# A fifth Strassen pair and three held pairs in the second FFN product of a two-layer trunk

## The chip, the core and the metric

The kernel runs on one core of one Trainium2 chip. The engines of a core work side by side, each on its own instruction stream: TensorE (PE; PEld is its weight load), VectorE (DVE), ScalarE (ACT), GpSimd (POOL), and SyncE (SP), which here issues the weight transfers. Matmul results go to eight banks of PSUM; everything else stands in SBUF. The metric is the device time of one execution in microseconds, as the median of several runs.

## What is computed

Two layers, each of three blocks on x of 256 tokens by 1024 channels, in float32:

```
for l in range(DEPTH):                                   # DEPTH = 2
    h = _swiglu(x, ffn_w1[l, 0], ffn_w3[l, 0], ffn_w2[l, 0])
    x = _layernorm(ALPHA * x + 0.5 * h, ln_g[l, 0], ln_b[l, 0])
    h = _mixer(x, ...)
    x = _layernorm(ALPHA * x + h, ln_g[l, 1], ln_b[l, 1])
    h = _swiglu(x, ffn_w1[l, 1], ffn_w3[l, 1], ffn_w2[l, 1])
    x = _layernorm(ALPHA * x + 0.5 * h, ln_g[l, 2], ln_b[l, 2])
```

with `_swiglu(x, w1, w3, w2) = (silu(x @ w1) * (x @ w3)) @ w2` and an inner width of 2816. The mixer (a gated spatial unit and differential attention, merged by gates) isn't touched by the change; what matters of it is that it starts, like an FFN, with a matrix product of the new x.

So there are four FFNs. Three of them hand their result to a next stage: to the mixer, to the next layer's first FFN, to the mixer again. The fourth ends the kernel.

## The kernel before

**Number format.** Every float32 operand is split into hi and lo: ACT copies it to the rounded type fp32r (hi), DVE subtracts hi from it (lo). A product then takes three matmuls, x_hi w_hi, x_hi w_lo and x_lo w_hi (`three`, L208). Weights arrive by DMA in pieces of 1 MB into `raw` (four buffers) and are split into `hi` and `lo` (eight buffers of 1024 columns each) by `stream` (L150). With `lent`, a half of a piece goes to slots of the activation pool instead (31 slots of 512 columns, the pool `act`), in splits of `sub` columns.

**An FFN** (L551) has two parts. The first makes the inner activations: four of the 22 k tiles (tiles of 128 inner channels) by `front`, the other 18 by `gemm_a2` in a loop over pairs of k tiles (L596). Inner tiles are kept as hi and lo, or, for pairs in `SQ`, go through `mixed` (L559), which adds and subtracts their 128 by 128 quarters for Strassen's form and splits the seven results.

The second part multiplies by w2 to 256 tokens by 1024 channels, in four blocks (t, c): token half t, channel half c. It goes by pairs of k tiles:

- a *plain pair* (`PQ`, `rows_p`): two k tiles in four blocks, three matmuls of 128x512 each. One `rows_p` call does one pair in one block, six matmuls;
- a *Strassen pair* (`SQ`, `stream_s` and L632): two k tiles, two token halves and two channel halves form a two by two block product, which takes seven block products S1 to S7 instead of eight, three matmuls each. `stream_s` (L280) forms the sums of weight blocks in place in `raw` (L306, L308, L309, on DVE) and splits seven blocks of 512 columns (`cut`, L289). Two pairs share one buffer for S1's weights.

Before the change there are four Strassen pairs and seven plain ones (`NS = 4`). The loop at L629 does a Strassen pair and, behind the first three, a plain pair. Then the sums of S1, S5, S6 and S7 go into the residual (L636 to L645, DVE), and the four plain pairs left are *held*: all are split into the eight `hi` and `lo` buffers, and the loop at L648 goes block by block, (0, 0), (0, 1), (1, 0), (1, 1), through all held pairs, so that a token half is done before the other.

**The normalization** (`Norm`, L434) follows each block: `part` adds a block to the residual, `finish(t, ...)` computes mean and variance of a token half and normalizes it on DVE (the last instruction is noted in `ends[t]`). For each half h of the channels, `turn(t, h)` (L528) then transposes on PE (L532), scales on ACT (L538) and splits the next stage's x on ACT and DVE (L540). For t = 0 and h = 1 DVE's part of the split is queued behind `ends[1]`, if that is set already.

**The order.** PE's instructions run in the order in which the program is traced. The other engines' order comes from a scheduler by priorities; `behind(ins)` puts an instruction behind `ins` on the same engine. Where PE does a transpose for a task is set by a beat counter: `beat(w)` (L123) is called with 0.5 for every `rows_p` or `rows_b` call and starts the tasks that are due; `finish` registers its task, which counts from the beat after it.

```
yield waits[h]            # turned(t, waits), L517
self.turn(t, h)
...
beat(n / 1024)            # rows_p, L258
...
ln.finish(t, ((2, 1.5), (2, 1))[t])      # the FFN, L655
```

**The next stage** begins with `gemm_b2` (L317): pieces of weights in steps of two k tiles (`rows_b`, six matmuls each), for t = 0 and then t = 1; x's first half (h = 0) is read by the first four steps, the second by the next four. Its four weight pieces are streamed with `lent = [(0, 1), (0,), (), ()]`, so that three halves go to slots.

## Time and profile before

| | us |
|---|---|
| median of 3 runs (1230.62 to 1231.16) | 1230.86 |
| the profiled execution | 1231.23 |
| its span, first to last instruction | 1229.5 |
| `wlo` splits on DVE (L171), 410 in all | 450.0 busy |
| `slo` splits on DVE (L295), 64 in all | 69.3 busy |
| sums of weight blocks on DVE (L306, L308, L309) | 19.6, 11.0, 11.0 busy |

Times are from the profile of one execution on the chip. In a row of a group, the name of the line and engine comes first, then the result and the operands, the shape and the count; behind the bar stand the time in which the engine was busy with the group, the mean of one in ns, and the idle time of the engine just before them with what ended it. In the timeline and in the chain of work that ended last, a row begins with its start and its length in us. In the table by stretches of time, each engine has its busy time and its number of instructions. Matmuls overlap, so a matmul's own length (390 ns) is more than the distance from one to the next.

### The profile page before, as it was taken

How to read it: one execution, taken by the hardware profiler on the slowest of the kernel's cores; microseconds unless marked ns; L12 is line 12 of the kernel's file. 1: busy time of each engine (PE TensorE's matmuls, PEld its weight loads, DVE VectorE, ACT ScalarE, POOL GpSimd, SP SyncE). 2: the span in 40 equal slices, each digit the busy share in tenths (PEclk: the TensorE clock that was granted, in tenths of full speed). 3: DMA queues.
4: the chain of work that ended last, by engine and by line, in shares of the span. 5: the costliest groups of instructions: out<-in, count | busy, mean ns of one | idle time of the engine just before them, and what ended most of it. 6: DMA issues, size and time to landing. Idle time of an engine off the chain costs nothing.

```text
span 1229.5 us, 17890 instructions
## 1 busy us (share of the span) xinstructions
PE 1223.3 (99%) x6589; PEld 1050.6 (85%) x6589; DVE 980.3 (80%) x1692; ACT 781.1 (64%) x1424; POOL 87.0 (7%) x184
## 2 busy tenths in 40 slices
PE   9999999999999999999999999999999999999998
PEld 8888888888888888888888888888888888888886
DVE  6877998886587987779978779978866879787886
ACT  6775666679665666656566665566886555766651
POOL 0100000244100000000000000002430000000000
PEclk9999999999999999999999999999999999999999
DMA  9864665654754745546645546656556446455450
GB/s 344 291 205 138 231 217 194 224 167 166 251 178 154 231 159 207 191 138 241 247 178 196 180 142 247 246 188 206 168 174 229 168 171 240 171 206 178 160 211 34
DMA packets 40104, 241.87 MB, mean 197 GB/s; under 512 B 5281, under 2 KB 6353, under 8 KB 13393
## 3 DMA queue, kind: packets, MB, share of 16 engines
q1 hardware_dynamic: 36048, 227.82, 53.2%
q0 software_dynamic: 3536, 12.13, 3.1%
q8 instruction: 51, 0.84, 0.3%
q10 hardware_dynamic: 432, 0.79, 0.2%
q14 instruction: 37, 0.30, 0.1%
HBM read 235.47 MB, written 1.05 MB: 192 GB/s over the span
## 4 chain that ended last, share of the span: by engine, by line
PE 99%; DMA 0%; DVE 0%; ACT 0%; DVEq 0%; issue 0%; ACTq 0%
PE bank L223 38%; PE bank L211 23%; PE bank L230 20%; PE sbank L211 12%; PE bank L371 2%; PE sbank L707 1%; PE sbank L532 1%; PE sbank L756 1%; PE sbank L837 1%; DMA xraw<-in_xT 0%; PE sbank L754 0%; PE sbank L778 0%; PE sbank L585 0%; PE sbank L741 0%; PE sbank L746 0%; PE sbank L504 0%
## 5 line engine op out<-in xcount | busy, mean ns | idle before, releaser
L171 DVE TENSOR_TENSOR wlo<-raw,whi 128x1024 fp32r<-128x1024 f32 (+1 forms) x410 | 450.0, 1116 | 109.1 <-PE bank L230 62.9
L169 ACT ACTIVATE whi<-raw 128x1024 fp32r<-128x1024 f32 (+1 forms) x410 | 388.8, 970 | 186.9 <-PE bank L223 114.8
L223 PE MATMUL bank<-x,whi 128*128 128x512 f32 x1792 | 426.5, 392 | 0.0
L223 PEld LDWEIGHTS bank<-x,whi 128*128 128x128 f32 x1792 | 330.7, 188 | 69.1 <-issue 2.7
L230 PE MATMUL bank<-x,wlo 128*128 128x256 f32 x1792 | 230.0, 284 | 0.0
L230 PEld LDWEIGHTS bank<-x,wlo 128*128 128x128 f32 x1792 | 224.2, 191 | 4.8
L231 ACT ACTIVATE r<-bank 128x256 f32<-128x256 f32 x256 | 96.0, 381 | 67.8 <-PE bank L230 67.4
L211 PE MATMUL bank<-whi,x 128*128 128x512 f32 x328 | 106.6, 394 | 0.0
L293 ACT ACTIVATE shi<-raw 128x1024 fp32r<-128x1024 f32 (+1 forms) x64 | 60.4, 950 | 61.0 <-DVE raw L309 39.1
L295 DVE TENSOR_TENSOR slo<-raw,shi 128x1024 fp32r<-128x1024 f32 (+1 forms) x64 | 69.3, 1088 | 24.8 <-PE bank L230 15.3
L211 PEld LDWEIGHTS bank<-whi,x 128*128 128x128 f32 x328 | 61.6, 188 | 12.7
L211 PE MATMUL sbank<-whi,hhi 128*128 128x512 f32 x168 | 65.7, 391 | 0.0
L211 PE MATMUL sbank<-whi,hlo 128*128 128x512 f32 x168 | 65.4, 389 | 0.0
L211 PE MATMUL sbank<-wlo,hhi 128*128 128x512 f32 x168 | 65.4, 389 | 0.0
L211 PE MATMUL bank<-wlo,x 128*128 128x512 f32 x164 | 64.0, 390 | 0.0
L538 ACT ACTIVATE xf<-sbank,ln_b,ln_g 128x128 f32<-128x128 f32 x80 | 30.1, 456 | 40.8 <-PE sbank L532 40.8
L233 DVE TENSOR_TENSOR silu<-bank,r 128x256 f32<-128x256 f32 x144 | 54.5, 418 | 0.4
L431 POOL DMA_DIRECT2D bc<-in_lng x6 | 3.2, 530 | 728.4 <-DVE bc L430 728.4
L683 POOL TENSOR_TENSOR swap<-swap,sin_t 128x512 f32<-128x512 f32 x16 | 25.0, 1563 | 233.4 <-DMA swap<-z 225.2
L211 PE MATMUL bank<-lhi,x 128*128 128x512 f32 x120 | 39.2, 395 | 0.0
L211 PEld LDWEIGHTS sbank<-whi,hlo 128*128 128x128 f32 x168 | 31.5, 188 | 6.7
L211 PEld LDWEIGHTS sbank<-wlo,hhi 128*128 128x128 f32 x168 | 31.6, 188 | 6.5
(236 smaller groups left out, 1682.3 us busy)
## 6 DMA issues: line engine op xcount, KB each, us to landing
raw<-in_w13a SPq DMA_DIRECT2D x72, 1024.0 KB, 4.9
raw<-in_w2p SPq DMA_DIRECT2D x28, 1024.0 KB, 5.1
raw<-in_wa SPq DMA_DIRECT2D x24, 1024.0 KB, 5.2
raw<-in_w2s SPq DMA_DIRECT2D x16, 1024.0 KB, 4.9
raw<-in_wb SPq DMA_DIRECT2D x16, 1024.0 KB, 5.0
raw<-in_wqk SPq DMA_DIRECT2D x16, 1024.0 KB, 5.2
raw<-in_wbr SPq DMA_DIRECT2D x16, 1024.0 KB, 4.9
raw<-in_w13b SPq DMA_DIRECT2D x12, 1024.0 KB, 5.1
```

What stands on the lines that cost most here:

```text
L169: A.activation(h, r, AF.Copy)
L171: V.tensor_tensor(out=w, in0=r, in1=h.bitcast(F32), op=ALU.subtract)
L211: PE.matmul(ps, xx, w, start=start and n == 0, stop=stop and n == 2)
L223: PE.matmul(b[-1], hi[:, k * P : (k + 1) * P], xc(k), start=k == 0, stop=False)
L230: PE.matmul(b[n][:, :T], lo[:, k * P : (k + 1) * P], xc(k)[:, :T], start=False, stop=k == KT - 1)
L231: emptied[0] = A.activation(r[:, s], b[n][:, T:], AF.Copy, scale=scale).ins
L233: a = V.tensor_tensor(out=z[:, s], in0=b[n][:, :T], in1=r[:, s], op=ALU.add)
L293: A.activation(h, r, AF.Copy)
L295: V.tensor_tensor(out=w, in0=r, in1=h.bitcast(F32), op=ALU.subtract)
L371: PE.matmul(ps[t][m], x[:, j, o + t * P : o + (t + 1) * P], y, start=k0 + j == 0 and o == 0 and y is hi, stop=k0 + j == KT - 1 and y is lo)
L538: A.activation(xf[:, s], b[:, s], AF.Identity, scale=self.gT[:, f], bias=self.bT[:, f])
L683: turned_by[0] = G.tensor_tensor(out=s3, in0=s3, in1=s, op=ALU.mult).ins
```

## The change

`NS` becomes 5: the pair (12, 13) goes from `PQ` to `SQ`, and six plain pairs are left. In the second part of an FFN the plain pairs stand behind the second, third and fourth Strassen pair instead of the first, second and third, so that the first two Strassen pairs follow each other, and three pairs are held instead of four. The first two of the held pairs are split into slots of the activation pool (in pieces of 512 columns), which the operands of finished Strassen pairs gave back; only the third uses `hi` and `lo`. In turn the stage after an FFN streams all its first weights to `hi` and `lo`: `ln.lent` is empty, while a mixer's `Norm` keeps the lent slots. In the first part of an FFN the product of a plain pair is now made and split for both tiles together. `stream` gets a parameter `dma`, which no call sets.

```diff
-NS = 4
+NS = 5
...
     def rows_p(ps, t, q, piece, xh, xl, c0=0, n=512, stop=False, start=False):
...
-            wh, wl = (v[:, j * 512 + c0 : j * 512 + c0 + n] for v in piece)
+            wh, wl = (v[j][:, c0 : c0 + n] if isinstance(v, list) else v[:, j * 512 + c0 : j * 512 + c0 + n] for v in piece)
...
         if norm:
-            lent = [(0, 1), (0,), (), ()]
+            lent = norm.lent
...
             self.ends, self.xlo = [None] * NT, {}
+            self.lent = [(0, 1), (0,), (), ()]
...
+        p_hi, p_lo = h_hi, h_lo
...
         for j in range(FB, FT, 2):
+            qa = s512("qa")
             for m, z in gemm_a2([w13a[l, f, j - FB + m] for m in range(2)], both, lambda m: t512("silu")):
                 s = z[:, :T]
                 silu[0] = A.activation(s, s, AF.Silu).ins
-                if (j, j + 1) in SQ:
-                    if m == 0:
-                        qa = s512("qa")
-                    V.tensor_tensor(out=qa[:, m * T : (m + 1) * T], in0=s, in1=z[:, T:], op=ALU.mult)
-                    if m:
-                        mixed((j, j + 1), qa)
-                else:
-                    V.tensor_tensor(out=s, in0=s, in1=z[:, T:], op=ALU.mult)
-                    split(hh(j + m), hl(j + m), s)
+                V.tensor_tensor(out=qa[:, m * T : (m + 1) * T], in0=s, in1=z[:, T:], op=ALU.mult)
+                if m and (j, j + 1) in SQ:
+                    mixed((j, j + 1), qa)
+                elif m:
+                    split(p_hi[j, j + 1], p_lo[j, j + 1], qa)
...
+        ln = Norm(l, i, 2.0 * ALPHA, 4.0 * EPS, qa[:, :1], last)
+        ln.lent = [()] * 4
...
         def plain_pair(hold):
             q = plain.pop(0)
-            w = stream(w2p[l, f, PQ.index(q)])
+            slot = hold and len(plain) > 0
+            w = stream(w2p[l, f, PQ.index(q)], sub=512 if slot else HC, lent=(0, 1) if slot else ())
...
-            if n < NS - 1:
+            if n in (1, 2, 3):
                 plain_pair(False)
```

More of the change, by code (lines that the diff above doesn't have):

```diff
@@ L148, in behind, with stream @@
         return tc.issue_after(ins) if ins is not None else nullcontext()
-    def stream(src, width=CH, sub=HC, lent=(), after=(None, None)):
+    def stream(src, width=CH, sub=HC, lent=(), after=(None, None), dma=()):
         step()
@@ L169, in stream @@
                     A.activation(h, r, AF.Copy)
+                if o // HC in dma:
+                    A.activation(w, r, AF.Copy, scale=-1.0)
+                    G.dma_start(w, src[:, o + p : o + p + sub], accum_op=ALU.add)
+                    continue
                 with behind(after[o // HC] or latest[1]):
@@ L599, in ffn @@
                 silu[0] = A.activation(s, s, AF.Silu).ins
-                if (j, j + 1) in SQ:
-                    if m == 0:
-                        qa = s512("qa")
-                    V.tensor_tensor(out=qa[:, m * T : (m + 1) * T], in0=s, in1=z[:, T:], op=ALU.mult)
-                    if m:
-                        mixed((j, j + 1), qa)
-                else:
-                    V.tensor_tensor(out=s, in0=s, in1=z[:, T:], op=ALU.mult)
-                    split(hh(j + m), hl(j + m), s)
+                V.tensor_tensor(out=qa[:, m * T : (m + 1) * T], in0=s, in1=z[:, T:], op=ALU.mult)
[3 more added lines that the diff above has]
+                    split(p_hi[j, j + 1], p_lo[j, j + 1], qa)
                 if norm is None and j + m == FB:
-                    beside(setup(s[:, :1]), 0)
-        ln = Norm(l, i, 2.0 * ALPHA, 4.0 * EPS, s[:, :1], last)
+                    beside(setup(qa[:, :1]), 0)
+        ln = Norm(l, i, 2.0 * ALPHA, 4.0 * EPS, qa[:, :1], last)
+        ln.lent = [()] * 4
         S = {n: side_bank() for n in (3, 7, 4)}
```

## The prediction

> **What bounds the kernel now.** I read the page first.

> ```profile
> PE 1223.3 (99%) x6589; PEld 1050.6 (85%) x6589; DVE 980.3 (80%) x1692; ACT 781.1 (64%) x1424; POOL 87.0 (7%) x184
> PEclk9999999999999999999999999999999999999999
> PE 99%; DMA 0%; DVE 0%; ACT 0%; DVEq 0%; issue 0%; ACTq 0%
> ```

> TensorE is busy in 99% of the span at the full clock, and the chain that ended last is PE for 99% of it. That alone doesn't exclude short waits, so the view of PE's waits comes next. It has four rows with 2.6 us in all; the two longest are

> ```profile
> PE sbank L383 <- DVE warm L379: 1.0, 1, 1.0
> PE sbank L500 <- DVE xtok L479: 1.0, 1, 1.0
> ```

> One lies before the first real matmul, the other in the tail. In between PE waits for nobody: the time is the number of matmuls times their spacing. So work taken from PE counts in full, work given to another engine counts nothing while PE's data is early, and each lateness counts in full, since no slack absorbs it. I therefore need the spacing, and how early the data is where the change touches it. The chain in order of time, at the first FFN's end (start, length, matmuls):

> ```profile
> 169.38 12.24 PE sbank L211 x54
> 181.62 0.44 PE sbank L532 x4
> 182.06 4.14 PE sbank L211 x18
> 186.20 0.44 PE sbank L532 x4
> 186.63 6.86 PE bank L211 x30
> ```

> 12.24 / 54 is **0.2267 us** a matmul. The 54 are 24 of block (0, 1), 24 of (1, 0) and 6 of (1, 1). Then come the four transposes of turn(0, 0), 18 matmuls, the transposes of turn(0, 1), and the next stage. I call one rows_p or rows_b call, six matmuls and 1.36 us, a step.

> **The change part by part.**

> *Matmuls.* A plain pair takes 2 x 2 x 2 x 3 = 24 matmuls, a Strassen pair 7 x 3 = 21. One pair is converted in each of four FFNs: 12 matmuls go, 12 x 0.2267 = **-2.72 us**. PE neither issues nor transposes anything new.

> *Vector and scalar work.* These rows (by form) price it.

> ```profile
> L295 DVE TENSOR_TENSOR slo<-raw,shi 128x1024 fp32r<-128x1024 f32 x48 | 58.3, 1221 | 9.6 <-ACT shi L293 9.6
> L306 DVE TENSOR_TENSOR raw<-raw 128x1024 f32<-128x1024 f32 x16 | 19.6, 1222 | 0.4
> L308 DVE TENSOR_TENSOR raw<-raw 128x512 f32<-128x512 f32 x16 | 11.0, 688 | 0.1
> 155.88 3.49 DVE L171 TENSOR_TENSOR wlo<-raw,whi 128x1024 fp32r<-128x1024 f32 x3
> 182.27 3.08 DVE L171 TENSOR_TENSOR wlo<-raw,whi 128x512 fp32r<-128x512 f32 x5
> ```

> Back to back, ends overlap: 3.49 / 3 is 1.14 us for 1024 columns (1.16 with the last one's tail), and 0.60 for 512. A Strassen pair costs DVE three splits and one sum of 1024, and one split and two sums of 512: 4 x 1.14 + 3 x 0.60 = 6.36 us against 4.76 us of PE; a plain pair 2.28 against 5.44. So an FFN gives DVE 4.1 us more, and mixed() three sums more. In slots a held pair is four splits of 512, 2.40 instead of 2.28. The merged split of plain products (one of 512 instead of two of 256) is a little cheaper. All of it is hidden if DVE keeps its lead:

> ```profile
> 128.39:163.90 35.51, 35.51 (x159) 29.42 (x158) 31.71 (x40) 20.01 (x26) 1.06 (x2) 1.00 0.73 262
> 135.70 1.23 DVE L295 TENSOR_TENSOR slo<-raw,shi 128x1024 fp32r<-128x1024 f32 x1 [1.19 <-ACT shi L293]
> 138.62 0.39 PE L211 MATMUL sbank<-shi,shh 128*128 128x512 f32 x1
> ```

> From the first block product to the last one DVE is busy 31.71 of 35.51 us. The second Strassen pair's last split ends at 136.93; PE wants it at that pair's eighth matmul, 138.62 + 7 x 0.2267 = 140.21: a lead of 3.28 us. Now no plain pair stands before it: PE comes 5.44 us sooner, and DVE has 2.28 us less in front. The lead is 3.28 - 5.44 + 2.28 = 0.12 us, and the 1.19 us that DVE idled there for ACT can be filled: up to 1.3. Afterwards plain and Strassen pairs alternate, 8.64 us of DVE in 10.20 of PE, so the lead grows. I take **0** for this, bounds 0 and the rival's price below. Below nothing isn't possible, as PE waits for no split today.

> *DMAs.* As many, of 1 MB, as before (one w2s for one w2p in each FFN), on the same SP queue:

> ```profile
> raw<-in_w2p SPq DMA_DIRECT2D x28, 1024.0 KB, 5.1
> raw<-in_w2s SPq DMA_DIRECT2D x16, 1024.0 KB, 4.9
> ```

> The first w2p moves behind the second w2s. Landing takes 5 us, and four raw buffers hold the loads some pairs ahead, about 5 us of PE each: nothing. A held pair in slots needs eight; 31 - 28 are free and each finished Strassen pair returns four, so the second has its eight when the fourth Strassen pair ends, 5.44 + 4.76 = 10.2 us before the held blocks begin. With hi and lo buffers free sooner, the next stage needs no lent slots: nothing on PE.

> *The hand-over.* Here the change has a cost that it doesn't name. finish(0) stands behind block (0, 1), and its task transposes x when beats have passed: start at the next step, plus 2 beats (four steps), plus 1.5 (three steps). So turn(0, 0) comes five steps after block (0, 1), and turn(0, 1) eight. With four held pairs a block is four steps, and eight follow: turn(0, 0) has three steps behind it, turn(0, 1) none, as the chain above shows. With three held pairs six follow: **one step stands between turn(0, 0) and the next stage**, whose first matmul reads x(0, 0). How long x takes:

> ```profile
> 181.81 0.48 PE L211 MATMUL sbank<-whi,hhi 128*128 128x512 f32 x1
> 182.20 1.49 ACT L538 ACTIVATE xf<-sbank,ln_b,ln_g 128x128 f32<-128x128 f32 x4
> 183.57 0.64 ACT L169 ACTIVATE whi<-raw 128x512 fp32r<-128x512 f32 x1
> 184.09 0.64 ACT L176 ACTIVATE x<-xf 128x512 fp32r<-128x512 f32 x1
> 185.27 0.69 DVE L177 TENSOR_TENSOR x<-xf,x 128x512 fp32r<-128x512 f32 x1
> 186.04 0.60 PE L532 MATMUL sbank<-ident,xtok 128*128 128x128 f32 x4
> ```

> ```profile
> 191.88 1.00 DVE L488 TENSOR_SCALAR xtok<-xtok,mv,nwy 128x512 f32<-128x512 f32 x2
> 193.68 0.49 PE L211 MATMUL bank<-whi,x 128*128 128x512 f32 x1
> 195.50 0.63 ACT L176 ACTIVATE x<-xf 128x512 fp32r<-128x512 f32 x1
> 196.16 0.69 DVE L177 TENSOR_TENSOR x<-xf,x 128x512 fp32r<-128x512 f32 x1 [2.68 <-ACT x L176]
> ```

> Counted from the first matmul behind the transposes, undisturbed (turn(1, 0), second fence) hi is there after 196.13 - 193.68 = 2.45 us and lo after 3.17. At turn(0, 0) (first fence) a weight split slips into ACT and hi takes 2.91; DVE is at weight splits too and lo takes 4.15. Today 18 matmuls, 186.04 - 181.81 = 4.23 us, and the next transposes cover that. One step covers 4.23 - 12 x 0.2267 = 1.51. The third matmul of the next stage, the first to read lo, would start at 1.51 + 0.45 = 1.96. After a wait its weight load goes first:

> ```profile
> 1222.98 0.41 DVE L479 TENSOR_TENSOR xtok<-xtok,bc 128x256 f32<-128x256 f32 x1
> 1223.44 0.30 PEld L500 LDWEIGHTS sbank<-xtok,ident 128*128 128x128 f32 x2 [1.80 <-DVE xtok L479]
> L211 PEld LDWEIGHTS bank<-whi,x 128*128 128x128 f32 x328 | 61.6, 188 | 12.7
> ```

> 1223.44 - 1223.39 = 0.05 from release to load, 0.19 for the load. So PE stands still for lo + 0.24 - 1.96: 1.45 us by the undisturbed row, 2.43 by the disturbed one. Behind the waiting matmul all of PE is queued. I take 1.92, for the disturbed hi (2.91) with an undisturbed lo (0.73 later): more buffers are free so that DVE's weight splits come sooner, but a split freed by the last held pair still falls into ACT's gap.

> turn(0, 1) falls two steps into the next stage, with two steps (4.23 - 6 x 0.2267 = 2.87 us) before its reader; lo is wanted by 2.87 + 0.45 - 0.24 = 3.08 and takes 3.17 undisturbed: 0.1, bounds 0 and 0.3. (Its split also comes to stand behind ends[1] on DVE, since finish(1) is now traced first. That ended at 192.88, 6.7 us after the last held matmul at 186.20; hi arrives 1.92 + 3.07 + 2.45 = 7.4 after it, so it decides nothing.) This happens at three hand-overs, as the last FFN has none: 3 x (1.92 + 0.1) = **+6.06 us**, bounds 3 x 1.45 = 4.35 and 3 x 2.73 = 8.2.

> *Sum:* -2.72 + 6.06 = **+3.3 us**, bounds +1.6 and +5.5. The profiled execution took 1231.23 (span 1229.5 and 1.73 around it), 0.37 above the median of 1230.86; that difference I leave out and add to the median: **1234.2 us**, own range 1232.5 to 1236.3.

> **The rivals.**

> *A, the hand-over is covered.* Then -2.72 alone: 1228.1. For it: only four scalings and one split lie between transposes and reader. Against it: today's 2.45 and 3.17 are with both engines idle before x, so waiting can't be shorter, and PE takes its order from the program. It decides where x(0, 0)'s lo comes within 1.72 us of the first matmul behind the transposes; or where beats fall otherwise than I count. Covered in part it would be no change. Chance 0.12, faster in 0.09 of it.

> *B, DVE loses its lead in the Strassen blocks.* The computed lead is 0.12 us. One 1024 split put ahead of the second pair's last one turns it to -1.02, in each of four FFNs: 4.1 us more, 1238.3. For it: 31.71 of 35.51 busy, and the order on DVE isn't written out by hand. Against it: 1.19 us of idle time, and PE's zero waits today. Chance 0.19.

> *C, TensorE's clock falls at the new waits.* If the 30 matmuls after each ran at half speed, 3 x 6.86 us more: 1254.8. Against it: today's 1.0 us wait before L500 left the granted clock at 1.000 in the view of cores:

> ```profile
> core 0: 1229.5 us, clock 1.000
> ```

> Chance 0.03. [...]

> **How the numbers follow.** My forecast has 0.66, with 0.17 of it under 0.2% (2.46 us, about what a measurement of this kernel can tell from no change: 1233.3), when the waits are near their lower bound. Slower: 0.49 + 0.19 + 0.03 = 0.71; same: 0.17 + 0.03 = 0.20; faster: 0.09. The range is to leave out A and C and the far end of B: 1230.0 to 1238.5.

> **What would show it.** PE's matmuls: 6589 - 12 = 6577. PE's waits: new rows of L211 for x, on ACT L176 and DVE L177, three each, 0.8 to 1.6 and 0.2 to 0.8 us long, right behind the one step that follows turn(0, 0). In the chain, x6 between turn(0, 0) and the next stage instead of x18. No waits for shi or slo; those would be B. If PE has no new waits, my count of beats is wrong, and the time is A's.

## The result and the profile after

The changed kernel takes **1246.43 us** (median of 4 runs, 1245.35 to 1247.12), the kernel before 1231.01 beside it: 1.0124 times as long, 95% interval 1.0108 to 1.014. It is slower, as forecast, but by 15.4 us instead of 3.3, and outside the range. The profiled execution took 1245.35, the shortest of the four, with a span of 1243.6, which is 14.1 more than before's 1229.5. Line numbers of the changed kernel are 4 or 5 higher: L211 is L215, L295 is L299, L176 and L177 are L180 and L181, L532 is L537, L488 is L493.

The page of the changed kernel, the same three lines as before:

```profile
PE 1227.2 (99%) x6577; PEld 1048.2 (84%) x6577; DVE 1003.3 (81%) x1724; ACT 787.1 (63%) x1432; POOL 85.8 (7%) x184
PEclk9999999999999999999999999999999999999999
PE 86%; DVE 8%; DMA 2%; ACT 2%; issue 1%; POOL 1%; SPq 0%; DVEq 0%; ACTq 0%; POOLq 0%
```

PE still shows 99% and the row of the clock is still all nines; neither gives the loss away. The 12 matmuls are gone (6577), and the chain that ended last now runs through DVE, DMA and ACT for 12% of the span. PE's waits (total, times, longest, in us) tell where:

```profile
PE bank L215 <- ACT x L180: 3.9, 3, 1.3
PE sbank L215 <- DVE slo L299: 3.0, 4, 0.8
PE bank L215 <- DVE x L181: 1.8, 3, 0.6
PE sbank L387 <- DVE warm L383: 1.0, 1, 1.0
PE sbank L505 <- DVE xtok L484: 1.0, 1, 1.0
PE bank L375 <- ACT whi L180: 0.8, 1, 0.8
PE sbank L215 <- ACT shi L297: 0.6, 1, 0.6
PE sbank L712 <- DVE hb L789: 0.3, 1, 0.3
```

Rows 1 and 3 are the forecast ones, three hand-overs each. Rows 2 and 7 are rival B: Strassen blocks that wait for their weights, once in each of the four FFNs.

Where the 14.1 us lie comes out of the start times of the same matmuls in both traces, from the first block product of an FFN to the transposes of turn(1, 1), and from there to the next turn(0, 0):

| stretch | before | after | more |
|---|---|---|---|
| to the first block product | 128.39 | 128.27 | -0.12 |
| FFN 1 | 68.16 | 71.39 | 3.23 |
| FFN 2 | 68.16 | 71.68 | 3.52 |
| FFN 3 | 68.16 | 72.78 | 4.62 |
| FFN 4, to the tail's transposes | 57.15 | 58.63 | 1.48 |
| the two mixers | 230.04, 230.06 | 230.51, 230.97 | 0.47, 0.91 |

**The hand-over** after FFN 1, PE's timeline in the changed kernel (start, length; in brackets the wait and its releaser), and DVE's at the same time:

```profile
184.74 0.66 PE L537 MATMUL sbank<-ident,xtok 128*128 128x128 f32 x4
185.16 0.48 PE L215 MATMUL sbank<-whi,hhi 128*128 128x512 f32 x1
186.40 0.40 PE L215 MATMUL sbank<-whi,hlo 128*128 128x512 f32 x1
188.08 0.50 PE L215 MATMUL bank<-whi,x 128*128 128x512 f32 x1 [1.29 <-ACT x L180]
188.42 0.40 PE L215 MATMUL bank<-wlo,x 128*128 128x512 f32 x1
189.41 0.73 PE L215 MATMUL bank<-whi,x 128*128 128x512 f32 x2 [0.59 <-DVE x L181]
```

```profile
184.16 0.99 DVE L493 TENSOR_SCALAR xtok<-xtok,mv,nwy 128x512 f32<-128x512 f32 x2
185.06 3.70 DVE L175 TENSOR_TENSOR wlo<-raw,whi 128x512 fp32r<-128x512 f32 x6
188.67 0.69 DVE L181 TENSOR_TENSOR x<-xf,x 128x512 fp32r<-128x512 f32 x1
```

One step of six matmuls stands between the transposes and the next stage, as forecast. From start to start, less 0.2267, PE loses 186.40 to 188.08 = 1.45 for hi, 0.11 on the matmul behind it, 0.76 for lo (188.42 to 189.41), and 0.11 again: 2.4 us. Lo is there 189.36 - 185.16 = 4.20 us after the first matmul behind the transposes, since six weight splits of the next stage stand ahead of it on DVE. That is the forecast's disturbed row (4.15), not the undisturbed one (3.17).

**The third Strassen pair** of FFN 1, timelines of SP's queue, ACT, DVE and PE:

```profile
132.60 0.33 SPq L288 DMA_DIRECT2D raw<-in_w2s  x1
```

```profile
139.66 1.58 ACT L297 ACTIVATE shi<-raw 128x512 fp32r<-128x512 f32 x2 [4.15 <-DMA raw<-in_w2s]
```

```profile
140.33 0.69 DVE L299 TENSOR_TENSOR slo<-raw,shi 128x512 fp32r<-128x512 f32 x1 [1.67 <-ACT shi L297]
140.93 0.69 DVE L312 TENSOR_TENSOR raw<-raw 128x512 f32<-128x512 f32 x1
141.54 1.22 DVE L299 TENSOR_TENSOR slo<-raw,shi 128x1024 fp32r<-128x1024 f32 x1
142.67 0.69 DVE L313 TENSOR_TENSOR raw<-raw 128x512 f32<-128x512 f32 x1
143.27 1.22 DVE L310 TENSOR_TENSOR raw<-raw 128x1024 f32<-128x1024 f32 x1
144.57 1.23 DVE L299 TENSOR_TENSOR slo<-raw,shi 128x1024 fp32r<-128x1024 f32 x1
```

```profile
144.62 0.47 PE L215 MATMUL sbank<-shi,shh 128*128 128x512 f32 x1
145.85 0.50 PE L215 MATMUL sbank<-slo,shh 128*128 128x512 f32 x1 [0.76 <-DVE slo L299]
```

The split at 140.33 belongs to the *fourth* pair, and so does the sum L310 at 143.27. The scheduler put that split ahead of the third pair's sums L312 and L313 and its last split (144.57), for which PE then waits: 144.62 to 145.85 is 1.00 us more than 0.2267. The fourth pair's load was issued only at 132.60 and landed at 139.6; ACT stood still for 4.15 us behind it and DVE for 1.67 us, with work of the third pair queued behind. It is the same in the second and third FFN, where DVE idles for 1.85 and 1.56 us. In the fourth the third pair's own first split comes late (1187.03, 10.1 us behind the first block product instead of 7.4) and DVE doesn't idle before the fourth pair's, but that split and sum stand ahead of the third pair's last split there too (1189.90 and 1192.92 ahead of 1194.21).

The kernel before has this order as well, in all four FFNs. Its third pair in FFN 1, on DVE:

```profile
144.58 0.68 DVE L295 TENSOR_TENSOR slo<-raw,shi 128x512 fp32r<-128x512 f32 x1
145.30 1.22 DVE L306 TENSOR_TENSOR raw<-raw 128x1024 f32<-128x1024 f32 x1
146.44 1.22 DVE L295 TENSOR_TENSOR slo<-raw,shi 128x1024 fp32r<-128x1024 f32 x1
```

The first two rows are the fourth pair's first split and sum, the last is the third pair's last split. It ends at 147.66, PE reads it at 150.40: a lead of 2.74 us, enough there.

**The clock** falls as well: the mean granted clock is 0.998 in the profile and 0.997 to 0.999 in the other runs, against 1.000 in the profile of before and 0.999 or 1.000 in its other runs. In stretches of 3.41 us behind the third hand-over (PE's busy time and matmuls, granted clock, DMA share, GB/s):

```profile
802.56:805.97 3.41, 1.51 (x6) 1.00 0.79 255
805.97:809.38 3.41, 3.41 (x10) 0.50 0.87 360
809.38:812.79 3.41, 3.41 (x19) 1.00 0.00 0
```

turn(0, 1) comes 7.07 us behind turn(0, 0) at the first two hand-overs and 8.59 at the third: about 1.5 us for this one stretch.

### The profile page after: what moved, and what is told of

It reads as the page before. It is cut to its first block, busy times and chain, and to the rows that moved or that the text cites. A ratio compares the mean times of both kernels' runs of the same rounds, so it can differ in the third digit from the quotient of the medians.

```text
span 1243.6 us, 17959 instructions
## 1 busy us (share of the span) xinstructions
PE 1227.2 (99%) x6577; PEld 1048.2 (84%) x6577; DVE 1003.3 (81%) x1724; ACT 787.1 (63%) x1432; POOL 85.8 (7%) x184
## 4 chain that ended last, share of the span: by engine, by line
PE 86%; DVE 8%; DMA 2%; ACT 2%; issue 1%; POOL 1%; SPq 0%; DVEq 0%; ACTq 0%; POOLq 0%
PE bank L227 37%; PE bank L215 20%; PE bank L234 19%; PE sbank L215 5%; DVE wlo L175 2%; PE bank L375 2%; DVE slo L299 2%; DMA raw<-in_w2s 1%; PE sbank L712 1%; ACT shi L297 1%; PE sbank L537 1%; PE sbank L842 1%; DVE xtok L477 0%; ACT whi L169 0%; PE sbank L761 0%
## 5 line engine op out<-in xcount | busy, mean ns | idle before, releaser
L175 DVE TENSOR_TENSOR wlo<-raw,whi 128x1024 fp32r<-128x1024 f32 (+1 forms) x404 | 434.9, 1094 | 92.8 <-PE bank L234 49.3
L169 ACT ACTIVATE whi<-raw 128x1024 fp32r<-128x1024 f32 (+1 forms) x404 | 375.0, 949 | 173.0 <-PE bank L227 116.2
L215 PE MATMUL bank<-whi,x 128*128 128x512 f32 x400 | 131.1, 399 | 5.7 <-ACT x L180 3.9
L299 DVE TENSOR_TENSOR slo<-raw,shi 128x1024 fp32r<-128x1024 f32 (+1 forms) x80 | 85.8, 1089 | 22.1 <-ACT shi L297 11.2
L215 PEld LDWEIGHTS bank<-whi,x 128*128 128x128 f32 x400 | 75.3, 189 | 24.0 <-ACT x L180 5.1
L215 PE MATMUL bank<-wlo,x 128*128 128x512 f32 x200 | 78.7, 393 | 0.0
L215 PEld LDWEIGHTS bank<-wlo,x 128*128 128x128 f32 x200 | 37.9, 190 | 7.3
L606 ACT ACTIVATE silu<-silu 128x256 f32<-128x256 f32 x72 | 29.5, 410 | 15.7 <-DVE silu L237 15.7
L215 PE MATMUL sbank<-whi,hhi 128*128 128x512 f32 x96 | 37.6, 392 | 0.0
L215 PE MATMUL sbank<-whi,hlo 128*128 128x512 f32 x96 | 37.4, 389 | 0.0
L215 PE MATMUL sbank<-wlo,hhi 128*128 128x512 f32 x96 | 37.4, 389 | 0.0
L722 ACT ACTIVATE pp<-pp,mx 128x256 f32<-128x256 f32 (+1 forms) x64 | 28.3, 444 | 13.6 <-DVE mx L720 13.6
## 6 DMA issues: line engine op xcount, KB each, us to landing
raw<-in_w13a SPq DMA_DIRECT2D x72, 1024.0 KB, 5.0
raw<-in_w2p SPq DMA_DIRECT2D x24, 1024.0 KB, 5.0
raw<-in_wa SPq DMA_DIRECT2D x24, 1024.0 KB, 5.2
raw<-in_w2s SPq DMA_DIRECT2D x20, 1024.0 KB, 4.9
raw<-in_wb SPq DMA_DIRECT2D x16, 1024.0 KB, 5.0
raw<-in_wqk SPq DMA_DIRECT2D x16, 1024.0 KB, 4.9
raw<-in_wbr SPq DMA_DIRECT2D x16, 1024.0 KB, 4.9
raw<-in_w13b SPq DMA_DIRECT2D x12, 1024.0 KB, 5.1
```

The costliest lines, as they stand in the source:

```text
L169: A.activation(h, r, AF.Copy)
L175: V.tensor_tensor(out=w, in0=r, in1=h.bitcast(F32), op=ALU.subtract)
L215: PE.matmul(ps, xx, w, start=start and n == 0, stop=stop and n == 2)
L299: V.tensor_tensor(out=w, in0=r, in1=h.bitcast(F32), op=ALU.subtract)
L606: silu[0] = A.activation(s, s, AF.Silu).ins
L722: A.activation(p[:, s], p[:, s], AF.Exp, bias=mx[:, a], scale=-1.0, accum_out=sums[:, a])
```

## The experiments

Two theories first. **H, the hand-over:** three held pairs leave one step too few. **O, the order:** with two adjacent Strassen pairs at the start, a load that comes late for DVE's queue delays the pair before it. Their rival was that DVE simply has too much to do with a fifth pair.

**1. Three held pairs alone** (e1_three_held), in the kernel before (four Strassen pairs):

```diff
-            if n < NS - 1:
-                plain_pair(False)
+            plain_pair(False)
```

> The kernel before with one held pair moved into the loop (a plain pair behind the fourth Strassen pair too, three held); four Strassen pairs, no slots. First theory, the hand-over: it has one step instead of three between turn(0, 0) and the next stage, so PE waits for x at three hand-overs, on ACT about 1.45 us and on DVE 0.2 to 0.8 us, with restarts 1.9 to 2.5 us each: 1231.0 + 5.7 to 7.5 = 1236.7 to 1238.5, and up to 1.7 more for each stretch in which the clock falls. Rival, the fifth pair's vector work makes x late: with four pairs the waits are under 0.5 us each, and the time is under 1232.5.

Measured: 1236.57 us (1235.94 to 1237.29), 1.0045 times before, 1.003 to 1.006. That is a little under the range. There is no wait for a weight split, and the x waits are there (2.6 us on ACT, 0.4 on DVE) at a clock of 1.0. Three held pairs with what hangs on them cost 5.7 us, and the fifth pair isn't needed for it. By the stretches of the table, FFN 1 to 3 take 1.9, 1.5 and 1.5 us more, each mixer 0.47, and the fourth FFN, which hands nothing over, takes 57.15 as before.

**2. The order alone** (e2_pair_order). In the changed kernel, a Strassen pair's splits are queued behind the last split of the pair before, on ACT and on DVE:

```diff
-    def stream_s(src, pair):
+    def stream_s(src, pair, past=(None, None)):
...
-            with behind(latest[0]):
-                A.activation(h, r, AF.Copy)
-            with behind(latest[1]):
-                V.tensor_tensor(out=w, in0=r, in1=h.bitcast(F32), op=ALU.subtract)
+            with behind(past[0] or latest[0]):
+                x = A.activation(h, r, AF.Copy).ins
+            with behind(past[1] or latest[1]):
+                return x, V.tensor_tensor(out=w, in0=r, in1=h.bitcast(F32), op=ALU.subtract).ins
...
-        cut(d, 1024, 1024)
+        past = cut(d, 1024, 1024)
```

> The changed kernel with the splits of a Strassen pair queued on ACT and DVE behind the last split of the pair before it. First theory: the waits for slo at the third pair come from DVE's order, in which the fourth pair's first split, waiting for its load, stands in front of the third pair's sums; they go, 1.0 to 1.9 us in each of four FFNs, 4.9 us in all, and the time falls from 1246.4 to about 1241.5. Rival, DVE hasn't the time for two adjacent Strassen pairs in any order: the waits move to another block, and the time stays within 1 us of 1246.4.

Measured: 1235.73 us (1235.24 to 1237.89), 1.0042, 1.0027 to 1.0057. That is 10.7 less than the changed kernel, twice what I expected. No Strassen block waits any more, so DVE has room for five pairs, three of the plain ones held, when its queue is in the right order. The fourth pair's load is issued even later than in the changed kernel (134.01 against 132.60), so a late load alone costs nothing. The third pair's last split ends at 143.02 and is read at 144.59: a lead of 1.57 us. PE at the first hand-over:

```profile
186.41 0.50 PE L215 MATMUL bank<-whi,x 128*128 128x512 f32 x1 [1.29 <-ACT x L180]
187.42 0.73 PE L215 MATMUL bank<-whi,x 128*128 128x512 f32 x2 [0.28 <-DVE x L181]
```

The wait for hi is the same (from 184.73 on), the one for lo 0.44 instead of 0.76 from start to start. The rest of the surprise lies in things that went with the late blocks: the half-clock stretch (1.5 us) and the transposes' waits for LN at turn(0, 0) (0.7 us in three FFNs) are gone.

**3. x ahead of the weights at the hand-over** (e3_x_first), in the changed kernel:

```diff
-            after[1:3] = (None, norm.ends[0]), (norm.ends[0], norm.ends[0])
+            e = norm.ends[0] if norm.lent[0] else norm.xlo[0, 0]
+            after[1:3] = (None, e), (e, e)
```

> The changed kernel with six weight splits of the next stage queued on DVE behind the split of x(0, 0) instead of behind ends[0], at the three hand-overs of an FFN. First theory: of the 2.4 us at a hand-over, 0.7 to 1.0 is DVE's queue and the rest is the way through PE, ACT and DVE; the wait on DVE falls from 0.78 to under 0.25 us, the one on ACT stays at 1.45, 1.5 to 3 us less in all: 1243.4 to 1244.9. Rival, the hand-over is late because normalization ends late: the order behind it changes nothing, 1246.4 within 0.7.

Measured: 1249.39 us (1248.39 to 1251.07), 1.0154, 1.0137 to 1.0171: a miss, and slower. One row of PE's waits and two of DVE's timeline say why:

```profile
PE bank L215 <- DVE x L181: 5.5, 3, 1.8
```

```profile
194.98 1.01 DVE L494 TENSOR_SCALAR xtok<-xtok,mv,nwy 128x512 f32<-128x512 f32 x2
195.90 0.69 DVE L181 TENSOR_TENSOR x<-xf,x 128x512 fp32r<-128x512 f32 x1
```

The first lo came in time, but the weight splits that gave way now alternate with LN of the second token half. That ended at 196 instead of 194, and x(0, 1)'s lo stands behind it by order (`ends[1]`), so the wait moved to the second half, 1.8 us long. DVE's work at the hand-over can be moved about, not saved.

**4. Unused matmuls in the gap** (e4_fill). Seven matmuls into a spare bank (1.6 us) in front of the next stage at the three hand-overs, nothing of the computation changed:

```diff
             ln.finish(t, ((2, 1.5), (2, 1))[t])
+        if not last:
+            idle = side_bank()
+            for _ in range(7):
+                PE.matmul(idle, hh(FT - 1)[:, :P], held[-1][1][1][0][:, :512], start=True, stop=True)
```

> The changed kernel with seven extra matmuls of 128x512 (1.6 us, their result unused) on PE at each of the three hand-overs, in front of the next stage. First theory: PE is waiting there anyway, so they cost nothing, the waits shrink by as much, and as PE is never idle long, the granted clock stays at 1.000, which gives back what the half-clock stretches cost: 1243 to 1246.4. Rival, PE isn't waiting for x but working: 3 x 1.6 us more, 1251.

Measured: 1241.94 us (1241.29 to 1244.38), 1.0092, 1.0077 to 1.0107. Twenty-one matmuls more, 4.76 us of PE, and 4.5 us less time, which is below the range of the theory. The x waits leave the list, the slo waits stay (3.0 us, 4) and those for shi grow from 0.6 to 1.1. So the gaps were idle as the list says. Two things come on top: the profile has no half-clock stretch before the tail, and the order around the gap isn't quite the same. On ACT x's hi (187.16) now comes ahead of the weight split that had stood in front of it, and DVE has five weight splits in front of lo instead of six, so the seven matmuls, 1.6 us, and one restart are all that is left of what had cost 2.4.

**5. The order and the fill together** (e7_order_fill): the edits of 2 and 4.

> The kernel of e2 with the seven extra matmuls of e4 at each hand-over. First theory: PE's waits there are pure waiting for x, so the fill costs nothing: 1234.8 to 1235.7, with the clock at 1.000 in every run and no run above 1236.5. Rival, the fill delays the next stage: up to 4.8 us more.

Measured: 1234.15 us (1233.77 to 1234.91, 10 runs), 1.0024, 1.0014 to 1.0034: 0.65 under the range, no run above 1236.5. PE's waits hold only those of the start and the tail. Counted from the kernel before beside it (1231.21), 12 matmuls fewer (-2.72) and 21 more (+4.76) make 1233.2; the remaining 0.9 us is no wait that the list shows. It lies in the two mixers, 0.49 and 0.44 us longer than before's.

**6. The plain pairs in their old places** (e8_old_places), in the changed kernel without the order of 2:

```diff
-            if n in (1, 2, 3):
+            if n in (0, 1, 2):
```

> The changed kernel with its three plain pairs of the loop in their old places, behind the first, second and third Strassen pair; the last two Strassen pairs are adjacent instead of the first two; order by the scheduler, three held. If the waits for slo come from two adjacent pairs at the start, they go there and come back, if at all, at the fifth pair; the hand-over keeps its 2.2 to 2.7 us three times: 1231.0 - 2.7 + 7 to 9 = 1235 to 1238 and up to 3 for the clock. If any late load of the next pair blocks DVE wherever the pairs stand, waits for slo of about 1 us an FFN remain and the time is 1240 to 1246.

Measured: 1236.16 us (1235.99 to 1236.63), 1.004, 1.0024 to 1.0056. One slo wait of 0.5 us is left, at the fifth pair of the fourth FFN. But the queue has not gone. DVE in FFN 1:

```profile
141.82 0.68 DVE L299 TENSOR_TENSOR slo<-raw,shi 128x512 fp32r<-128x512 f32 x1
144.16 1.22 DVE L310 TENSOR_TENSOR raw<-raw 128x1024 f32<-128x1024 f32 x1
145.29 1.22 DVE L299 TENSOR_TENSOR slo<-raw,shi 128x1024 fp32r<-128x1024 f32 x1
```

The fourth pair's first split and sum stand ahead of the third pair's last split here too. What differs is the time that PE leaves: with a plain pair more ahead of it the third pair begins at 148.42 instead of 143.26, DVE doesn't idle before 141.82, and the last split ends 3.50 us before PE reads it (146.51 and 150.01). So the two Strassen pairs at the start don't make the order, they take away the lead that had covered it.

**7 and 8. Four held pairs with the order of 2** (e5_order_four_held and e6_order_four_held_late), to give the hand-over its steps back: only two plain pairs in the loop, in 7 behind the second and fourth Strassen pair, in 8 behind the second and third.

```diff
-            if n in (1, 2, 3):
+            if n in (1, 3):
...
-            slot = hold and len(plain) > 0
+            slot = hold and len(plain) > 1
```

> Five Strassen pairs with the queue order of e2, and four held pairs again: plain pairs in the loop only behind the second and fourth Strassen pair, two held pairs in slots, two in hi and lo. First theory: with four steps to a block the hand-over has its old cover and no waits for x; in e2 the fourth pair's last split ended at 152.05 and was wanted at 154.80; without the plain pair before it PE comes 5.44 us sooner and DVE has 2.28 us less to do, so it is late by about 0.4 us an FFN: 1230.9 - 2.7 + 1.6 to 2.5 = 1229.8 to 1230.7. Rival, DVE loses more when two pairs are adjacent twice: waits for slo of 1 to 3 us an FFN, 1233 to 1240.

> As e5, but with the plain pairs behind the second and third Strassen pair, so that the last two Strassen pairs and the four held pairs follow each other. First theory: the fifth pair's last split was at 163.18 in e2 behind four slot splits (2.4 us) that can wait; wanted 5.44 us sooner, at about 159.6, it comes at 158.5, so no Strassen pair waits; if the held splits keep up, 1230.9 - 2.7 = 1228.2 to 1229.5. Rival, the held splits (9.4 us of DVE behind 158.5) and the sums of block products don't fit before PE needs the fourth held pair at 167.0: waits of 0.5 to 2 us an FFN, 1230.5 to 1236.

Measured: 1249.56 us (1248.68 to 1251.42), 1.0146, 1.0128 to 1.0164; and 1244.84 us (1244.23 to 1248.73), 1.0117, 1.0099 to 1.0134. Both miss by some 15 us or more, and both rivals by about 9. The x waits are gone, as H says. In 7 PE waits for slo (8.9 us, 9 times) and for splits of held pairs (7.3, 4), in 8 at the fifth pair:

```profile
PE sbank L215 <- DVE slo L299: 6.0, 5, 1.3
PE sbank L215 <- ACT shi L297: 4.2, 4, 1.1
```

A stretch of the first FFN in 8 (PE, PEld, DVE, ACT, POOL: busy time and instructions; clock, DMA share, GB/s), and rows of DVE's timeline in and behind it:

```profile
150.00:160.60 10.60, 9.55 (x43) 7.46 (x41) 10.60 (x15) 6.86 (x10) 0.00 (x0) 1.00 0.49 160
```

```profile
159.23 0.68 DVE L175 TENSOR_TENSOR llo<-raw,lhi 128x512 fp32r<-128x512 f32 x1
160.43 0.68 DVE L175 TENSOR_TENSOR llo<-raw,lhi 128x512 fp32r<-128x512 f32 x1
161.03 1.22 DVE L299 TENSOR_TENSOR slo<-raw,shi 128x1024 fp32r<-128x1024 f32 x1
```

DVE is busy for all of the stretch, but not only with what PE wants next. Six slot splits of held pairs (`llo`, 148.73 to 160.43, 0.60 us each: 3.6 us) stand ahead of the fifth pair's last split at 161.03, and PE loses 2.8 us at that pair. The expectation had taken them as splits "that can wait"; nothing in the edit makes them wait. The question left was whether DVE's amount of work decides, or whether it is only late for another reason.

**9. Less work for DVE** (e10_less_sums): 8 without two of a Strassen pair's three sums (0.69 us each), so the block products that need them are not the reference's.

```diff
-        V.tensor_tensor(out=raw[:, 1024:1536], in0=raw[:, :512], in1=raw[:, 1024:1536], op=ALU.add)
-        V.tensor_tensor(out=raw[:, 1536:], in0=raw[:, 1024:1536], in1=raw[:, 1536:], op=ALU.add)
```

> e6_order_four_held_late (four held pairs, pair order, 1244.84 us) with two of the three sums of a Strassen pair (the two 128x512 sums, 0.69 us each on VectorE) left out, so that the block products of these weights are not the reference's. Theory: with four held pairs VectorE is full from the third pair on, and its work is what the fifth pair waits for; 1.2 to 1.4 us less in each of five pairs is more than the 2.75 us of those waits: no wait for slo or shi above 0.3 us at the fifth pair, no wait for x, no half clock there, 1227.8 to 1230.0. Rival: the loads or the order of the queues set the fifth pair's time, and VectorE is only full because it is behind: 1238 or more.

Measured: 1228.77 us (nine of ten runs 1228.12 to 1229.33, one 1292.21), 0.998 times before, 0.997 to 0.9989. All waits in the blocks and at the hand-over are gone:

```profile
127.60:160.00 32.40, 32.40 (x145) 26.64 (x144) 29.55 (x37) 20.79 (x29) 1.06 (x2) 1.00 0.65 227
```

PE is busy in all of 32.40 us. With less work on DVE four held pairs run without a wait, and the 12 matmuls are worth about what was counted, 2.3 us by the medians against 2.72. That the amount alone stands against four held pairs isn't shown: the edit also takes two links out of the chain from load to last split, and 8 with its held splits queued behind the fifth pair's last one was not tried.

**10. turn(0, 0) a step earlier** (e9_order_turn), with the order of 2:

```diff
-            ln.finish(t, ((2, 1.5), (2, 1))[t])
+            ln.finish(t, ((1.5, 1), (2, 1))[t])
```

The second number also shortens the way from turn(0, 0) to turn(0, 1) from three steps to two, so turn(0, 1) comes two steps earlier and now falls ahead of the next stage; the expectation doesn't count with that.

> The changed kernel with the pair order of e2_pair_order, and turn(0, 0) of the FFNs traced one step earlier (1.36 us), so that two steps instead of one stand between it and the next stage. Theory: the hand-over is one chain from block (0, 1) through LN(0), transposes and split to the next stage's first read, and six held steps are short of it by a fixed amount; the earlier transposes then wait for LN(0)'s scaling by about what the next stage waits less: 1234.8 to 1236.4, beside 1235.7 of e2_pair_order. Of PE's waits those for x shrink from about 1.3 to 0.2 us each and a wait of the transposes for xtok of 1.2 to 1.6 us each comes in. Rival: only the distance from the transposes to the reader counts, LN(0) being done in time: 1.3 us less at three hand-overs, 1231.2 to 1232.4.

Measured: 1233.07 us (1232.48 to 1233.85, 10 runs), 1.0016, 1.0006 to 1.0025: 2.7 less than 2, between the ranges of the two theories. Its PE waits:

```profile
PE sbank L537 <- DVE xtok L493: 3.4, 6, 0.7
```

The transposes wait for LN, as the theory of one chain has it, but at most 0.7 us each: x's hi on ACT (184.85) now comes ahead of a weight split, and lo on DVE (185.52) stands behind four of them instead of six. How much of the 2.7 us is turn(0, 1)'s was not separated. Three of the six waits are new ones at turn(1, 0), because the weight splits delay LN of the second half in their turn.

**11 and 12. turn(1, 0) and turn(1, 1) a step later** as well (e11_order_turn_late), to take those three waits out; in 12 (e12_order_turn_spread) turn(0, 1) too, by `(1.5, 1.5)`.

```diff
-            ln.finish(t, ((1.5, 1), (2, 1))[t])
+            ln.finish(t, ((1.5, 1), (2.5, 1))[t])
```

> e9_order_turn (1233.07 us) with turn(1, 0) and turn(1, 1) of the FFNs traced one step (1.36 us) later, so that they come behind LN(1)'s scaling. Theory: the 0.60 to 0.65 us that the transposes of turn(1, 0) wait for LN(1) at three hand-overs are taken by the step that now stands ahead of them, and x(1, 0) still arrives 0.2 us ahead of its reader: 1230.8 to 1231.8, level with the kernel before, the 0.76 to 0.89 us at turn(0, 0) staying. Rival: the wait moves to the reader of x(1, 0), which has one step less: 1232.4 to 1233.6.

> e11_order_turn_late with turn(0, 1) one step later as well. Theory: turn(0, 1) has time to spare (its lo is there 3.8 us after its transposes, its reader more than two steps behind them), so that the same comes out, 1230.8 to 1231.8. Rival: x(0, 1)'s lo then stands behind LN(1)'s work on VectorE and is late: 1232 to 1235.

Measured: 1233.7 us (1233.32 to 1234.61), 1.0025, 1.0015 to 1.0035; and 1234.47 us (1234.03 to 1237.11), 1.0033, 1.0023 to 1.0043. Both theories missed; 11 came just above its rival's range, 12 inside its rival's, but without the wait for x(0, 1) that the rival names. In 11 the waits at turn(1, 0) are gone, and in their place a mixer waits:

```profile
PE sbank L537 <- DVE xtok L493: 2.1, 3, 0.8
PE sbank L712 <- ACT aT L748: 1.1, 2, 0.6
```

Why the mixer's scores come late there was not traced further. No version with the whole computation was faster than the kernel before; 10 comes nearest.

## Why the prediction was wrong, point by point

**The matmuls:** right. 6577, and -2.72 us stands, as 9 shows.

**The Strassen blocks: the step that failed.** I put the waits in the blocks at 0, because I worked DVE's lead out from amounts of work: 0.12 to 1.3 us at the second pair, and "Afterwards plain and Strassen pairs alternate, 8.64 us of DVE in 10.20 of PE, so the lead grows". The second pair did hold. It was the third that waited, 1.0 to 1.1 us with the restart in each of the first three FFNs and 2.0 in the fourth, where ACT's half was late too, since DVE does not do the work in the order in which PE wants it: the fourth pair's first split and sum stand ahead of the third pair's last split, and where that split waits for its load, DVE stands still.

The trace of before would have told it. By the rule of amounts the lead of 3.28 us at its second pair should have grown by 10.20 - 8.64 = 1.56 at the third; it had fallen to 2.74, because the same split and sum, 1.74 us back to back, stood ahead there too. The changed kernel has a plain pair less ahead of the third pair, so 2.74 - 5.44 + 2.28 = -0.42 us: a wait at the third pair, by the prediction's own working, had it started from that row. In the changed kernel that split came 0.95 us late (145.80 against 143.26 + 7 x 0.2267). With the order pinned down (2) the lead there is 1.57, close to the 0.12 + 1.56 that the amounts give. Rival B had the mechanism (a split put ahead of a pair's last one) and a fair price, 1.0 us an FFN, but at the second pair and with a chance of 0.19. In the trace of the changed kernel DVE stood idle for 1.67 us ahead of 140.33 while the third pair's sum L312, whose inputs were there from 138.66 on, stood behind the split.

**The DMAs "nothing": wrong in one place.** I counted loads and buffers and took landing at 5 us. The fourth pair's load was issued only at 132.60 and was there 7 us later. That by itself would have held nothing up, as 2 shows with a load issued at 134.01; it did because the queue put its reader first and PE was close behind. 2 takes away the first of these and 6 the second, and 10.7 and 10.3 us go with them.

**The hand-over:** the mechanism and its place were right, and 1 shows it alone. The size was inside the bounds: 1.92 + 0.1 forecast for each, 2.4 in the changed kernel, and 2.1 in 2 (1.46 + 0.44 and two restarts of 0.11). I mixed a disturbed hi with an undisturbed lo, 3.64 us behind the first matmul; with the weight splits put ahead of x on DVE lo was disturbed as well and came after 4.20, in 2 after 3.88. The extra 0.1 at turn(0, 1) was not there. That 2 comes so close to the forecast is in part luck: lo was later than assumed, and the 0.1 fell away.

**"So it decides nothing"** of the order behind `ends[1]`: right for the changed kernel, but with less room than it sounded. In 3 it decided, for 1.8 us each.

**Rival A:** refuted; the one step doesn't cover x.

**Rival C:** I gave the clock 0.03 and 6.86 us at each hand-over. Ahead of the tail it fell once in the profiled execution, to 0.50 for 3.41 us behind the third hand-over, at a cost of about 1.5 us; PE had waited 1.3 and 0.6 us in the stretch ahead of it (last section). Small, but a part of the miss.

**The sum.** Twelve matmuls -2.7; hand-overs 3 x 2.4 = +7.3; waits in the blocks with their restarts +5.3; the transposes' waits for LN +0.7; the half clock +1.5; the mixers +1.4 make 13.5 of the 14.1 us of the span. The mixers were not in the prediction's sum. About 0.47 us also lies in each mixer of 1, 2 and 5, at the first of its scores, and none in those of 8 and 9, which hold four pairs; so it hangs on three held pairs, and not on the waits for x, which 5 doesn't have. Of 10's two mixers the first has 0.02 and the second 0.70. Where it comes from stays open. With the order pinned down the time lies inside the forecast's range: 2 came to 1235.73, against 1234.2 and a range to 1238.5.

## What to carry to other kernels

A lead worked out from amounts of work holds only if the queue is in the order in which it is consumed: where a scheduler sets it, read the lead of each pair from the trace instead of one, look for the next load that comes late and ask what its reader will be put in front of, or pin the order down. Work that is held back until the end is not only work, it is the cover for the next hand-over; count the steps between the last transposes and their reader before you take one away. And where PE, DVE and the hand-over are all near their limit, 12 matmuls less on PE need not be worth anything: none of the versions with the whole computation gained by them, and 9, with less work on DVE, gained 2.3 us.

## What the runs showed of the hardware that was not expected

```profile
625.22:628.64 3.42, 1.62 (x8) 1.00 0.97 383
628.64:632.05 3.41, 3.39 (x17) 1.00 0.39 156
```

```profile
158.39:161.81 3.42, 1.60 (x6) 1.00 0.91 309
161.81:165.22 3.41, 2.92 (x7) 0.50 0.57 171
```

Outside the first and last microseconds, every stretch at full clock in which PE was busy for 1.60 us or less was followed by one at half clock (1.51, 1.57, 1.60, and 1.00 and 1.19 in 7 and 8), and none was with 1.62 or more, in the traces of before, the changed kernel and nine of the experiments (1 to 4, 6 to 8, 10 and 11). (In 8 a stretch at half clock with 2.40 us busy was followed by a second one.) So in these traces the share in a fixed stretch tells the two apart, with the border between 1.60 and 1.62 of 3.41 us, about 47%; the ends of matmuls in the profile are modelled, so the second decimal is not to be trusted. At the third hand-over the two waits of 1.3 and 0.6 us lay in one stretch and half clock followed; at the first two the same two waits were spread over two stretches (PE busy for 2.12 and 1.90 us in the lower one) and the clock stayed at 1.00.

**The waits at a hand-over cost more than their own length:** the start behind a matmul that had waited came 0.11 us late, as at 188.08 to 188.42 (0.34 instead of 0.2267), twice at each hand-over of the changed kernel.
